# Relaying out the delta rule's diagonal blocks on two DMA queues

## The chip, the cores and the metric

The kernel runs on one core of a Trainium2 chip. The core has five engines with a queue each: TensorE (PE in the profile; its weight loads are PEld), VectorE (DVE), ScalarE (ACT), GpSimd (POOL) and SyncE (SP), and DMA transfers that an engine's queue issues. An engine runs its own queue in order. The metric is the time of one execution in microseconds on the device; the median of repeated runs counts.

## The reference

Two transformer blocks, one after the other, on 512 tokens of width 1024, all in float32. The first block mixes by a gated delta rule (four heads) and a spatial gate, then attends to a memory of 256 rows, then runs an MLP. The second has an mLSTM and window attention, an MLP and a gated embedding. The change lies in the delta rule of the first block. Per head, the reference solves a unit lower triangular system in each chunk of 64 positions:

```python
m = jnp.where(strict, jnp.einsum('bhnid,bhnjd->bhnij', k_beta, k) * lmask, 0.0)
a = m + jnp.eye(c, dtype=f32)
rhs = jnp.concatenate([v_beta, k_beta * jnp.exp(decay)[..., None]], axis=-1)
sol = lax.linalg.triangular_solve(a, rhs, left_side=True, lower=True, unit_diagonal=True)
...
_, o = lax.scan(step, s0, xs)
```

## The kernel before

Every large product of float32 matrices is made of three matmuls on split operands (lines 284, 285 and 286, in the helper `mm3`): a high half rounded to a shorter float type (`wh`, made by a ScalarE cast, line 265) and the rest (`wl`, made by a VectorE subtraction, line 266). `wload` does this for each weight: a DMA on SyncE's queue into `wr` (line 261), the cast, the subtraction. The weights of one projection are two such loads, so TensorE cannot go on with a product before VectorE has made the second `wl`.

The kernel uses chunks of 128 positions for the delta rule, four of them (`NB`), and inverts the unit triangular matrix of each chunk explicitly. `dn_head` does one head in two steps, separated by a `yield`. The first normalises q and k (squares at lines 618 and 621, an inverse root by Newton steps on VectorE at lines 187 to 192), makes the decay factors (636 to 641) and the products `dM` and `QKT` (648, 651). The second inverts: it starts from the 16x16 blocks on the diagonal, 8 in each of 4 chunks, 32 in all.

The diagonal blocks are first gathered by a product with a mask (line 666 with a 16-wide result) and copied by ScalarE to `Lp` (line 676, tile `dVb`), in which the rows of the blocks lie along the 128 partitions. Four DMAs (line 683, one for each chunk) relay them out into `Lb` (in tile `dV`): 32 partitions, one block of 16x16 in each. There VectorE inverts all 32 blocks at once by 15 steps of two small instructions (lines 686 and 688) in `Tb`, and four more DMAs (line 690) bring the result back to the layout along the partitions, `Rp` (tile `dY`). Line 692 reads that into `dTb`. Two rounds of block merging follow (lines 666 four more times a head, 699, 700, 703, 706, 709), then the last merge to 128 (716 to 726), the products with the right sides (612), and a scan over the four chunks (740 to 759).

The four heads run beside the projections of the mixer and, from head 2 on, beside the projections of the memory (`xa_wk`, `xa_wv`), whose keys are made by 256-wide matmuls. The memory's rows come in by DMAs of line 818 on SyncE's queue. After a head, `L778` transposes its output for the projection that follows.

What stands where on each engine is not written out in the kernel. A scheduler sets it when the program is built, from the dependences and its own estimate of what takes how long. So a change of a queue in two lines may move instructions of all engines. At run time the order on an engine is fixed, and an instruction that waits holds what stands behind it.

Of the kernel before, what the change touches and what calls it, by code (L numbers as in the profile page):

```python
# [66 lines left out]
class Kern:  # L67
# [523 lines left out]
    def dn_head(self, h, q, k, v, pr, gate, yb_h, yb_l):  # L591

        nc, mp = self.nc, self.mp
# [81 lines left out]
        Lp, Rp = b32("dVb")[:, :, :16], b32("dY")[:, :, :16]  # L675
# [3 lines left out]
        Lb, Tb, Ob = bl(Vt, 0), bl(Vt, 256), bl(Mo, 0)  # L679
        V.memset(Tb, 0.0)  # L680
        V.memset(flat(Tb)[:, 0::17], 1.0)
        for b in range(NB):
            nc.sync.dma_start(Lb[8 * b:8 * b + 8], Lp[:, b])
        for j in range(15):
            n, m = 15 - j, j + 1
            nc.vector.tensor_tensor(out=Ob[:, :n, :m], in0=Lb[:, m:, j:m].broadcast_to([32, n, m]),
               in1=Tb[:, j:m, :m].broadcast_to([32, n, m]), op=ALU.mult)
            nc.vector.tensor_tensor(out=Tb[:, m:, :m], in0=Tb[:, m:, :m], in1=Ob[:, :n, :m], op=ALU.subtract)
        for b in range(NB):
            nc.sync.dma_start(Rp[:, b], Tb[8 * b:8 * b + 8])  # L690
        T_ = b32("dTb")
        TT(out=split(T_, 16), in0=split(Rp, 16).broadcast_to([P, NB, 2, 16]),
           in1=split(self.bmask("half"), 16).broadcast_to([P, NB, 2, 16]), op=ALU.mult)
# [940 lines left out]
```

## Time and profile before

| | us |
|---|---|
| median of three timed runs | 1692.23 (1691.33 to 1692.98) |
| profiled execution, whole | 1697.81 |
| its span | 1695.9 |
| DMAs of line 683, first and last start | 115.9, 225.5 |
| DMAs of line 690, first and last start | 135.2, 257.2 |
| key projections of the memory begin | 211.3 |

In the profile a row of an engine's timeline gives the start in us, the time taken, engine and line, the operation with the tile it writes and those it reads, shapes, and how many equal ones are merged; what stands in brackets is how long the engine was idle before it and what ended that. A matmul is pipelined, so its time overlaps with the next one's; a float32 matmul that is not split shows as two records. A row of waits gives the total in us, the times and the longest. A row of windows gives the stretch, its length, the busy time of TensorE, its weight loads, VectorE, ScalarE and GpSimd with counts, the granted clock of TensorE, the DMA engines' share and GB/s. "SPq" and "ACTq" are the issues on SyncE's and ScalarE's queues.

### The profile page before, as it was taken

To read this page: it belongs to the slowest core of one execution; us is meant where nothing else is said; L and a number is where in the kernel's file an instruction comes from. 1 tells how busy PE (TensorE), PEld (TensorE's weight loads), DVE (VectorE), ACT (ScalarE), POOL (GpSimd) and SP (SyncE) were. 2 spreads that over 40 slices of the span, in tenths; PEclk is the share of its full clock that TensorE was granted. 3 is DMA by queue.
4 is the path that set the end of the run, shared out by engine and by line. 5 is a ranking of instruction groups with operands and counts; after the bars stand their busy time and mean duration, and the time that the engine had idled before them with its cause. 6 is when DMAs were issued, how large, how long until landed. Compare 5 with 4: busy or idle time off the path is not lost.

```text
span 1695.9 us, 25881 instructions
## 1 busy us (share of the span) xinstructions
PE 1680.3 (99%) x9916; PEld 1462.6 (86%) x9916; DVE 1210.9 (71%) x2521; ACT 823.3 (49%) x1462; POOL 71.9 (4%) x92
## 2 busy tenths in 40 slices
PE   9999999999999999999999999999999999999998
PEld 8988899777898989899999887788888989898987
DVE  6988876756676867688856569865466767676875
ACT  5355745544444444455454457654244444444554
POOL 0200000100000000000000000000000000000000
PEclk9999989999999999999999999999999999999999
DMA  6321347636446464433333332334464464644331
GB/s 204 101 76 52 96 129 179 162 81 171 128 130 169 126 173 120 148 100 98 103 94 106 100 88 69 94 87 112 114 196 121 128 175 124 170 125 141 100 112 50
DMA packets 81947, 205.63 MB, mean 121 GB/s; under 512 B 13088, under 2 KB 14240, under 8 KB 81824
## 3 DMA queue, kind: packets, MB, share of 16 engines
q1 hardware_dynamic: 62672, 169.29, 31.9%
q0 software_dynamic: 9216, 16.78, 7.0%
q10 hardware_dynamic: 9936, 17.91, 3.8%
q8 instruction: 78, 1.28, 0.3%
q14 instruction: 45, 0.37, 0.1%
HBM read 201.59 MB, written 35.65 MB: 140 GB/s over the span
## 4 chain that ended last, share of the span: by engine, by line
PE 90%; DVE 5%; ACT 2%; DMA 1%; issue 1%; SPq 0%; ACTq 0%; DVEq 0%
PE psd L286 21%; PE psd L284 21%; PE psd L285 21%; PE x L284 6%; PE x L285 5%; PE x L286 5%; DVE wl L266 1%; PE c L666 1%; PE c L612 1%; PE lg L1375 1%; PE po L1402 1%; ACT wh L265 1%; DVE S L442 1%; DMA wr<-in_xa_wq_dram 0%; PE c L284 0%
## 5 line engine op out<-in xcount | busy, mean ns | idle before, releaser
L286 PE MATMUL psd<-S,wl 128*128 128x512 f32 (+1 forms) x1256 | 484.1, 386 | 2.7 <-DVE wl L266 2.5
L284 PE MATMUL psd<-S,wh 128*128 128x512 f32 (+1 forms) x1256 | 486.3, 388 | 0.0
L285 PE MATMUL psd<-S,wh 128*128 128x512 f32 (+1 forms) x1192 | 458.5, 385 | 0.5 <-DVE S L330 0.5
L286 PEld LDWEIGHTS psd<-S,wl 128*128 128x128 f32 x1256 | 237.9, 190 | 48.9 <-DVE wl L266 4.3
L284 PEld LDWEIGHTS psd<-S,wh 128*128 128x128 f32 x1256 | 238.5, 190 | 44.5 <-ACT S L326 0.4
L266 DVE TENSOR_TENSOR wl<-wr,wh 128x1024 fp32r<-128x1024 f32 (+2 forms) x160 | 192.1, 1201 | 110.0 <-ACT wh L265 109.2
L285 PEld LDWEIGHTS psd<-S,wh 128*128 128x128 f32 x1192 | 226.1, 190 | 43.3 <-DVE S L330 1.0
L265 ACT CAST wh<-wr 128x1024 fp32r<-128x1024 f32 (+2 forms) x160 | 163.9, 1026 | 149.1 <-PE psd L285 101.2
L284 PE MATMUL psd<-wh,S 128*128 128x256 f32 (+2 forms) x480 | 135.9, 283 | 0.0
L286 PE MATMUL psd<-wh,S 128*128 128x256 f32 (+2 forms) x480 | 135.6, 283 | 0.0
L285 PE MATMUL psd<-wl,S 128*128 128x256 f32 (+2 forms) x480 | 135.5, 282 | 0.0
L284 PE MATMUL x<-S,wh 128*128 128x256 f32 x452 | 129.0, 287 | 0.2
L285 PE MATMUL x<-S,wh 128*128 128x256 f32 x452 | 126.6, 281 | 0.0
L286 PE MATMUL x<-S,wl 128*128 128x256 f32 x452 | 126.0, 280 | 0.0
L284 PE MATMUL psd<-S,whx 128*128 128x512 f32 (+1 forms) x296 | 107.9, 366 | 0.0
L286 PE MATMUL psd<-S,wlx 128*128 128x512 f32 (+1 forms) x296 | 107.5, 364 | 0.0
L285 PE MATMUL psd<-S,whx 128*128 128x512 f32 (+1 forms) x296 | 107.2, 363 | 0.0
L1001 DVE TENSOR_TENSOR x_fm<-x_fm,x 128x256 f32<-128x256 f32 x192 | 79.7, 418 | 24.8 <-PE x L286 23.1
L284 PEld LDWEIGHTS psd<-wh,S 128*128 128x128 f32 x480 | 90.5, 189 | 0.4
L285 PEld LDWEIGHTS psd<-wl,S 128*128 128x128 f32 x480 | 90.4, 188 | 0.3
L284 PE MATMUL x<-S,whx 128*128 128x256 f32 x316 | 90.6, 287 | 0.0
L286 PEld LDWEIGHTS psd<-wh,S 128*128 128x128 f32 x480 | 90.4, 188 | 0.1
(455 smaller groups left out, 3174.7 us busy)
## 6 DMA issues: line engine op xcount, KB each, us to landing
wrx<-in_ffn_w_dram SPq DMA_DIRECT2D x32, 512.0 KB
wrx<-in_w_up_dram SPq DMA_DIRECT2D x20, 512.0 KB
wr<-in_w_in_qk_dram SPq DMA_DIRECT2D x16, 512.0 KB
sums_ffn_w<-in_ffn_w_dram ACTq DMA_DIRECT2D x32, 256.0 KB
wr<-in_ffn_w_dram SPq DMA_DIRECT2D x16, 512.0 KB
sums_w_down<-in_w_down_dram ACTq DMA_DIRECT2D x32, 256.0 KB
wr<-in_w_in_v_dram SPq DMA_DIRECT2D x12, 512.0 KB
wr<-in_w_up_dram SPq DMA_DIRECT2D x12, 512.0 KB
```

The source lines that it names most:

```text
L265: self.last_cast = nc.scalar.copy(hi[:, c], raw[:, c])
L266: nc.vector.tensor_tensor(out=lo[:, c], in0=raw[:, c], in1=hi[:, c].bitcast(F32), op=ALU.subtract)
L284: mm(ps, ah, bh, start=first, stop=False, skip_group_check=more)
L285: mm(ps, ah, bl, start=False, stop=False, skip_group_check=more)
L286: self.last_mm = mm(ps, al, bh, start=False, stop=last, skip_group_check=more)
L442: nc.vector.tensor_scalar(out=d, in0=d, scalar1=ag[:, j, 0:1], scalar2=r[:, j:j + 1], op0=ALU.subtract, op1=ALU.mult)
L612: nc.tensor.matmul(blk(ps, b), lhs(b), rhs(b), start=True, stop=True)
L666: nc.tensor.matmul(ps[:, b * n:(b + 1) * n], lhs[:, b], rhs(b), start=True, stop=True)
L1001: TT(out=x[n][t], in0=x[n][t], in1=ps, op=op)
L1375: nc.tensor.matmul(ps[:, i, K0:], qs[:, 2 * e2 + i, cs], kd[:, w, kc], start=(w == 0), stop=(w == 1))
L1402: nc.tensor.matmul(po, vhl[:, kb, j], pT[:, w], start=(kk == kks[0] and w == 0), stop=(kk == 1 and w == 1))
```

## The change

Of each group of four DMAs, the second and the fourth are issued from ScalarE's queue; the first and the third stay on SyncE's.

```diff
         for b in range(NB):
-            nc.sync.dma_start(Lb[8 * b:8 * b + 8], Lp[:, b])
+            (nc.scalar if b % 2 else nc.sync).dma_start(Lb[8 * b:8 * b + 8], Lp[:, b])
         for j in range(15):
...
         for b in range(NB):
-            nc.sync.dma_start(Rp[:, b], Tb[8 * b:8 * b + 8])
+            (nc.scalar if b % 2 else nc.sync).dma_start(Rp[:, b], Tb[8 * b:8 * b + 8])
```

Nothing is computed otherwise. The scheduler orders TensorE, VectorE, ScalarE and SyncE anew between about 108 and 300 us of the run; GpSimd's order is the same. Two places matter below.

The first is the start of the memory's key projection, beside heads 2 and 3. On SyncE's queue, with `wr` the weights of `xa_wk`, `e` the memory's rows, `dV` and `dY` the relays of head 2 (the last one, `dV_2835`, is head 3's):

```order
 L818 DMA e_491_2705<-in_mem_dram 128x256
 L818 DMA e_493_2712<-in_mem_dram 128x256
-L261 DMA wr_3024<-in_xa_wk_dram 128x1024
+L683 DMA dV_2283<-dVb_399_2280 8x16x16 x2
 L261 DMA wr_3030<-in_xa_wk_dram 128x1024
-L690 DMA dY_400_2281<-dV_2283 128x1x16 x4
 L261 DMA wr_3096<-in_xa_wk_dram 128x1024
-L683 DMA dV_2835<-dVb_518_2832 8x16x16 x4
 L261 DMA wr_3102<-in_xa_wk_dram 128x1024
+L690 DMA dY_400_2281<-dV_2283 128x1x16 x2
+L683 DMA dV_2835<-dVb_518_2832 8x16x16 x2
```

The write-back of head 2 moves from ahead of the weights `wr_3096` and `wr_3102` to behind them; `wr_3024` moves further ahead.

On VectorE at the same place, before; `wl_2756` is the lower half of the second weight of the first key projection, 686 and 688 are the inversion of head 2, whose fifteen steps run from 32x15 over 32x14x2 to 32x15 again:

```order
L686 TENSOR_TENSOR dA_402_2284<-dV_2283 32x3x13
L648 TENSOR_TENSOR dM_2576<-c_462_2571,slg_2546 128x512
L688 TENSOR_TENSOR dV_2283<-dV_2283,dA_402_2284 32x3x13
L651 TENSOR_TENSOR QKT_2583<-c_464_2578,slg_2546 128x512
L686 TENSOR_TENSOR dA_402_2284<-dV_2283 32x2x14
L190 TENSOR_TENSOR rsmt_2726<-rsmy_2725 128x2
L266 TENSOR_TENSOR wl_2756<-wr_2754,wh_2755 128x1024
L688 TENSOR_TENSOR dV_2283<-dV_2283,dA_402_2284 32x2x14
```

and now:

```order
L686 TENSOR_TENSOR dA_402_2284<-dV_2283 32x13x3
L191 SCALAR_TENSOR_TENSOR dot_1873<-dot_1873,dso_1860 128x4
L266 TENSOR_TENSOR wl_2756<-wr_2754,wh_2755 128x1024
L192 SCALAR_TENSOR_TENSOR doy_1872<-dot_1873,doy_1872 128x4
L688 TENSOR_TENSOR dV_2283<-dV_2283,dA_402_2284 32x13x3
L190 TENSOR_TENSOR dot_1873<-doy_1872 128x4
L475 TENSOR_TENSOR x_fm<-psd_2648,x_fm 128x512
```

The weight's lower half moves from the fourteenth step of the inversion to the third, and with it ahead of head 3's factors (641) and products (648, 651). `wl_3026` and `wl_3032`, the two of the second key projection, move from behind the inversion to its tenth and eleventh steps; `wl_3098`, of the third, stands behind the first L700 of head 2 in both orders, but now ahead of the L706 that follows, where the second L700 stood ahead of it.

The second place is head 2's write-back on ScalarE. `wh` are casts of weights, `S_503` the keys' high half, `vt` head 3's scaled values, `S_176` head 1's output, `dVb_518` head 3's diagonal blocks:

```order
 L643 ACTIVATE kdec_2561<-c_450_2515,dkd_2542 128x128 x3
+L265 CAST wh_3097<-wr_3096 128x1024
+L326 CAST S_503_2745<-e_514_2814 128x256
+L690 DMA dY_400_2281<-dV_2283 128x1x16 x2
 L643 ACTIVATE vt_2563<-c_466_2585,dvi_2544 128x128 x4
+L265 CAST wh_3103<-wr_3102 128x1024
 L329 ACTIVATE S_176_1231<-c_515_2818,vec 128x512
 L676 COPY dVb_518_2832<-c_517_2827 128x4x16
```

The two write-backs come in ahead of head 3's `vt`, and the casts of the third key projection's weights move from behind L676 to around them.

On TensorE, the groups of head 2's merging (L666, four products each; tiles `c`) stand among the key projection's matmuls (`psd`). Two of them before:

```order
L286 MATMUL psd_3065<-S_477_2662,wl_3026 128x256
L666 MATMUL c_407_2339<-dY_406_2337,dV_2283 128x32 x4
L284 MATMUL psd_3065<-S_477_2662,wh_3025 128x256
L285 MATMUL psd_3065<-S_478_2663,wh_3025 128x256
L286 MATMUL psd_3065<-S_477_2662,wl_3026 128x256
L284 MATMUL psd_3065<-S_477_2662,wh_3025 128x256
L285 MATMUL psd_3065<-S_478_2663,wh_3025 128x256
L286 MATMUL psd_3065<-S_477_2662,wl_3026 128x256
L284 MATMUL psd_3065<-S_477_2662,wh_3025 128x256
L666 MATMUL c_408_2345<-dTb_403_2325,dA_402_2284 128x32 x4
```

and now:

```order
L285 MATMUL psd_3137<-S_478_2663,wh_3097 128x256
L666 MATMUL c_407_2339<-dY_406_2337,dV_2283 128x32 x4
L286 MATMUL psd_3108<-S_477_2662,wl_3098 128x256
L284 MATMUL psd_3108<-S_477_2662,wh_3097 128x256
L285 MATMUL psd_3108<-S_478_2663,wh_3097 128x256
L666 MATMUL c_408_2345<-dTb_403_2325,dA_402_2284 128x32 x4
L286 MATMUL psd_3108<-S_477_2662,wl_3098 128x256
```

Between the two stand three matmuls where seven stood. In the whole run of head 3's first group (`c_517`, 16 wide) and head 2's four (`c_404`, `c_407`, `c_408`, `c_411`), the matmuls between neighbours are 4, 8, 3 and 10 now, and were 14, 11, 7 and 10; the transposes of L778 stand four matmuls ahead of `c_517` now, and stood next to it.

## The prediction

> **What bounds the kernel now.** I read the page first: busy shares, granted clock, chain.
>
> ```profile
> span 1695.9 us, 25881 instructions
> PE 1680.3 (99%) x9916; PEld 1462.6 (86%) x9916; DVE 1210.9 (71%) x2521; ACT 823.3 (49%) x1462; POOL 71.9 (4%) x92
> ...
> PEclk9999989999999999999999999999999999999999
> ...
> PE 90%; DVE 5%; ACT 2%; DMA 1%; issue 1%; SPq 0%; ACTq 0%; DVEq 0%
> ```
>
> TensorE works 1680.3 of 1695.9 us and carries 90% of the chain. The change removes no TensorE instruction. It can move the time in two ways only: through the 15.6 us in which TensorE stands, and through the one slice in which the clock digit is 8. So I asked for TensorE's own waits, and for the stretch around that digit in order of time.
>
> ```profile
> PE psd L286 <- DVE wl L266: 2.5, 3, 1.2
> ...
> PE c L666 <- DVE dTb L692: 0.2, 1, 0.2
> ```
>
> ```profile
> 214.52 1.15 PE L612 MATMUL c<-dq,dk 128*128 128x128 f32 x8
> 215.43 0.36 PE L284 MATMUL psd<-S,wh 128*128 128x256 f32 x1
> ...
> 217.74 0.39 PE L286 MATMUL psd<-S,wl 128*128 128x256 f32 x1 [1.16 <-DVE wl L266]
> ...
> 219.25 0.28 PE L285 MATMUL psd<-S,wh 128*128 128x256 f32 x1
> 219.37 0.28 PE L286 MATMUL psd<-S,wl 128*128 128x256 f32 x1
> ...
> 220.20 0.60 PE L778 MATMUL c<-masks,do 128*128 128x128 f32 x4
> 220.63 0.96 PE L666 MATMUL c<-masks,dT 128*128 128x16 f32 x8
> 221.44 0.36 PE L286 MATMUL psd<-S,wl 128*128 128x256 f32 x1
> ...
> 224.38 0.38 PE L286 MATMUL psd<-S,wl 128*128 128x256 f32 x1 [0.88 <-DVE wl L266]
> ...
> 224.74 1.08 PE L666 MATMUL c<-dTb,dT 128*128 128x32 f32 x8
> 225.65 0.39 PE L285 MATMUL psd<-S,wh 128*128 128x256 f32 x1
> ...
> 227.97 1.75 PE L666 MATMUL c<-dY,dV 128*128 128x32 f32 x8
> ```
>
> ```profile
> 210.00:220.00 10.00, 8.84 (x74) 8.57 (x74) 9.78 (x57) 4.29 (x13) 0.82 (x1) 1.00 0.30 65
> 222.20:225.60 3.40, 2.52 (x20) 2.10 (x18) 3.33 (x9) 1.38 (x3) 0.00 (x0) 1.00 0.47 157
> 225.60:239.20 13.60, 13.60 (x66) 13.60 (x66) 5.92 (x18) 4.50 (x10) 0.81 (x1) 0.51 0.46 119
> ```
>
> The first number is a start; the difference of two starts is what a row costs in a full stream (219.25 to 219.37: 0.12 us for a 256-wide matmul; 224.74 to 225.65: 0.91 for a group of four L666 products; 220.63 to 221.44: 0.81 for the 16-wide group; 220.20 to 220.63: 0.43 for four transposes; 214.52 to 215.43: 0.91 for four 128-wide products). Two waits of 1.16 and 0.88 us, both for the lower half of a split weight (`wl`, L266), fall into the key projection of the memory, beside head 2's inverse. VectorE, which makes `wl`, is busy 9.78 of 10 us there: it is late because it is full. Right after the second wait the granted clock drops to 0.51 for 13.6 us: (1 - 0.51) x 13.6 = 6.7 us lost. So this stretch holds 2.04 us of waits and 6.7 us of clock; that is what the change can win.
>
> **The change part by part.** Its direct effect is on 32 small transfers.
>
> ```profile
> L690 SPq DMA_DIRECT2D dY<-dV x16: 604/648/1817, 135.2 to 257.2; - x16
> ```
>
> ```profile
> 218.97 3.90 SPq L690 DMA_DIRECT2D dY<-dV  x4
> 223.04 0.34 SPq L261 DMA_DIRECT2D wr<-in_xa_wk_dram  x1
> ```
>
> ```profile
> 206.30 0.50 ACTq L226 DMA_DIRECT2D sums_ffn_w<-in_ffn_w_dram  x1
> 206.47 0.26 ACT L621 ACTIVATE c<-c 128x128 f32<-128x128 f32 x1
> ```
>
> One issue takes 0.648 us of SyncE. Two of four moved make each of the eight relays 2 x 0.648 = 1.3 us shorter. That is 10.4 us over all eight, none of it on TensorE's path: heads 0 to 3 run beside projections, and a reader of a relay (L692 to L666) kept TensorE waiting once, for 0.2 us. I cost it at zero; if the cover were gone it would be at most the 1.3 us of one relay at a time.
>
> ScalarE takes 16 issues in return. No row shows such a transfer on its queue; the nearest are 0.50 us for L226 there and 0.648 on SyncE, 8 to 10.4 us in all. An activation starts at 206.47 while L226's issue runs to 206.80, so an issue need not stop the engine; ScalarE is busy 49%. I take zero, bounds 0 and 1.3 us for the one place where ScalarE's work is next on TensorE's path (the slower rival).
>
> [...]
>
> What counts is the order that the shorter relays give to the engines.
>
> ```profile
> 213.47 0.33 DVE L641 SCALAR_TENSOR_TENSOR slg<-slg,ds,masks 128x128 f32<-128x128 f32 x1
> 213.73 0.20 DVE L688 TENSOR_TENSOR dV<-dV,dA 32x55 f32<-32x55 f32 x1
> ...
> 214.99 0.69 DVE L648 TENSOR_TENSOR dM<-c,slg 128x512 f32<-128x512 f32 x1
> 215.59 0.18 DVE L688 TENSOR_TENSOR dV<-dV,dA 32x39 f32<-32x39 f32 x1
> 215.71 0.69 DVE L651 TENSOR_TENSOR QKT<-c,slg 128x512 f32<-128x512 f32 x1
> ...
> 216.41 0.14 DVE L190 TENSOR_TENSOR rsmt<-rsmy 128x2 f32<-128x2 f32 x1
> 216.48 1.21 DVE L266 TENSOR_TENSOR wl<-wr,wh 128x1024 fp32r<-128x1024 f32 x1
> ...
> 218.81 0.10 DVE L688 TENSOR_TENSOR dV<-dV,dA 32x15 f32<-32x15 f32 x1
> ...
> 224.39 0.29 DVE L692 TENSOR_TENSOR dTb<-dY,masks 128x128 f32<-128x128 f32 x1
> ```
>
> By starts, an L641 costs 0.26 us, an L648, L651 or L475 0.6, an L686 or L688 about 0.13, one of the tiny ones (L187 to L192 and the like) 0.07. In the new order 60 VectorE instructions that stood ahead of `wl_2756` (the wait at 217.74) stand behind it: 22 of L686 and L688 (2.9 us), four L641 (1.0), L648, L651 and L475 (1.8), and 31 tiny ones (2.2). That is 7.9 us; two memsets (0.3) come ahead. On TensorE, what stood ahead of its first use shrinks by 16 matmuls of 0.12, three groups of 0.91 and the transposes of L606 (0.4): 5.1 us. Its margin grows by 7.6 - 5.1 = 2.5 us, more than the 1.16 it was late. For `wl_3032` (the wait at 224.38) VectorE sheds 5.8 us net and TensorE 2.6: 3.2 us of margin against 0.88. SyncE's issue at 223.04, a weight held up behind head 2's write-back, now stands ahead of it too. **Both waits go: -2.04 us.**
>
> What is late next is `wl_3098`. VectorE now makes it two places behind L700 (one L828 of 0.35, then 1.14), and TensorE wants it directly behind the group that itself needs L700 (0.91). If that group starts just as L700 ends, TensorE waits 0.35 + 1.14 - 0.91 = 0.6 us; if VectorE is ahead, nothing. I take **+0.5 us** (bounds 0, and 2.0 if as much is lost as now).
>
> Whether the clock falls again is the large question. Head 2's small groups stand closer: from the four transposes of L778 to the end of the last of five L666 groups there are 29 matmuls, 29 x 0.12 + 0.43 + 0.81 + 4 x 0.91 = 8.4 us, and 4.9 of these, 58%, are groups that stream little. Before the fall, of 222.2 to 225.6, wait, group and the two transposes of L360 took 0.88 + 0.91 + 0.2 of 3.4 us: also 58%. Head 1, where the clock held:
>
> ```profile
> 178.17 1.08 PE L666 MATMUL c<-dTb,dT 128*128 128x32 f32 x8
> ...
> 185.34 0.97 PE L666 MATMUL c<-dY,dV 128*128 128x32 f32 x8
> ```
>
> four groups and one of transposes in 8.1 us, (4 x 0.91 + 0.43) / 8.1 = 50%. The limit lies between; the new place is on the falling side. I let the fall **stay: 0** (bounds -6.7 and +6.7, gone or twice as long).
>
> Sum against the profiled execution's 1697.81 us (span and 1.9 around it): 1697.81 - 2.04 + 0.5 = 1696.3. The median of the timed runs is 5.6 us lower, at 1692.23; carried over, **1690.7 us**. Two runs are told from no change at about 0.2%, 3.4 us: this forecast is "same".
>
> **Rivals.** *A, the clock holds.* With the waits gone, no single place of the run has idle time and groups together; both earlier heads kept their clock. Against it: the 58%. It gives 1692.23 - 2.04 - 6.7 = 1683.5. [...]
>
> *B, slower: ScalarE waits.* At head 2 its two write-backs wait for VectorE's last L688; behind them on ScalarE stand `vt` (four scalings), the cast `wh_3103`, L329, L676 and L703, whose result the second L666 group reads:
>
> ```profile
> 216.50 1.14 ACT L643 ACTIVATE vt<-c,dvi 128x128 f32<-128x128 f32 x4 [2.04 <-PE c L606]
> 220.83 0.69 ACT L329 ACTIVATE S<-c,vec 128x512 fp32r<-128x512 f32 x1 [3.19 <-PE c L778]
> ...
> 221.74 1.05 ACT L265 CAST wh<-wr 128x1024 fp32r<-128x1024 f32 x1
> ```
>
> From the last L688 this path is about 1.3 (two issues) + 1.1 + 1.1 + 0.7 us, and some 0.4 for the two small copies: 4.6 us. Now that L688 ends at 218.9 and the group starts at 227.97; at full clock and without the wait that would be 226.8 - 0.9, 7.0 us later. The order adds 3.0 us of TensorE's work and 1.6 of VectorE's: 8.4 us against 4.6. It decides once the recursion ends nearly 4 us later than that; then TensorE idles amid the groups and the low clock lasts about twice as long: 1690.7 + 6.7 = 1697.4.
>
> *C, the relays get no shorter*, since their landing, not their issue, holds them. The order is fixed when the program is built, so the first two waits still go, and one relay 1.3 us late may show: 1692.23 - 2.04 + 1.3 = 1691.5.
>
> **How the numbers follow.** Forecast 0.45, A 0.30, B 0.13, C 0.12. Forecast and C are "same": 0.57; A is faster, 0.30; B slower, 0.13. The range runs from A's 1683.5, rounded down to 1683, to 1696, which takes the waits at their upper bound and a fall half as long again; B is left out. The likeliest case alone reaches from 1689 to 1694.
>
> **What would show it.** Right: no wait of L286 for `wl` over 0.5 us in the key projection, the chain of waits still 90% TensorE, one digit below 9 in the clock row, some 3 us later than now, with matmuls of 0.21 us between starts. Wrong: a clock row of nines (A); idle of TensorE at L666 for L703 or L692, and ScalarE idle before `vt` (B); issues of L683 and L690 that still take over 2 us from first to first reader with TensorE waiting at L666 (C). A fall beside head 0 or 1 would refute the 50 to 58%.

## The result, and the profile after

| | before | after |
|---|---|---|
| median of the runs, us | 1692.38 (1691.33 to 1692.98, 4 runs) | 1703.62 (1703.09 to 1704.51, 4 runs) |
| ratio of after to before | | 1.0069 (95% interval 1.0058 to 1.0081) |
| profiled execution, us | 1697.81 | 1704.51 |

The change makes the kernel slower by 0.7%, 11 us. I had forecast 1690.7 and a range of 1683 to 1696. First the page of the kernel after: span, busy time, granted clock in 40 slices, chain.

```profile
span 1702.7 us, 25884 instructions
...
PE 1682.9 (99%) x9916; PEld 1463.5 (86%) x9916; DVE 1210.6 (71%) x2521; ACT 823.7 (48%) x1462; POOL 71.9 (4%) x92
...
PEclk9999989999999999999999999999999999999999
...
PE 87%; DVE 7%; ACT 2%; DMA 2%; issue 1%; ACTq 0%; DVEq 0%; SPq 0%
```

It looks like the page before: TensorE carries the chain, one clock digit is below 9. Idle time of TensorE rose from 15.6 to 19.8 us. Its waits (total, times, longest) and three stretches of windows (the figure behind the five busy times is the granted clock):

```profile
PE c L666 <- DVE dTb L692: 2.3, 2, 2.0
PE c L666 <- ACT vt L643: 1.2, 1, 1.2
...
PE c L753 <- ACT do L755: 0.9, 1, 0.9
...
PE c L666 <- DVE doy L192: 0.8, 1, 0.8
...
PE psd L286 <- DVE wl L266: 0.7, 2, 0.5
```

```profile
180.00:190.00 10.00, 7.99 (x38) 6.50 (x38) 5.60 (x14) 5.14 (x19) 1.02 (x1) 0.83 0.53 123
230.00:240.00 10.00, 9.53 (x51) 9.33 (x52) 7.15 (x16) 3.04 (x8) 0.40 (x1) 0.63 0.40 97
240.00:250.00 10.00, 10.00 (x66) 9.21 (x65) 3.92 (x15) 4.11 (x8) 0.41 (x1) 0.69 0.36 81
```

The waits for `wl` went from 2.5 to 0.7 us, as forecast. New are a wait of 2.0 us for head 1's relay (L692), one of 1.2 us for `vt` at head 2, and two of 0.9 and 0.8 behind 240 us. And the clock is low at two places: beside head 1 (0.83 in 180 to 190) and beside head 2.

Head 1 in the timeline of after, queues, VectorE and TensorE together:

```profile
176.25 0.33 SPq L261 DMA_DIRECT2D wr<-in_xa_wk_dram  x1
...
176.54 1.36 ACTq L690 DMA_DIRECT2D dY<-dV  x2
...
176.68 1.44 SPq L690 DMA_DIRECT2D dY<-dV  x2
...
183.24 0.29 DVE L692 TENSOR_TENSOR dTb<-dY,masks 128x128 f32<-128x128 f32 x1 [2.29 <-DMA dY<-dV]
...
183.59 1.08 PE L666 MATMUL c<-dTb,dT 128*128 128x32 f32 x8 [2.01 <-DVE dTb L692]
```

All four write-backs were issued by 178.1, and the last of them landed only at 183.1. Ahead of SyncE's two stands a 512 KB weight, which the scheduler had put behind them before:

```profile
173.44 2.67 SPq L690 DMA_DIRECT2D dY<-dV  x4
...
176.71 1.56 SPq L261 DMA_DIRECT2D wr<-in_xa_wk_dram  x2
```

Head 2, first ScalarE, then TensorE:

```profile
227.43 1.05 ACT L265 CAST wh<-wr 128x1024 fp32r<-128x1024 f32 x1 [2.42 <-PE c L606]
227.53 1.45 ACTq L690 DMA_DIRECT2D dY<-dV  x2
228.38 0.40 ACT L326 CAST S<-e 128x256 fp32r<-128x256 f32 x1
229.03 1.14 ACT L643 ACTIVATE vt<-c,dvi 128x128 f32<-128x128 f32 x4 [0.24 <-issue]
```

```profile
230.22 1.06 PE L666 MATMUL c<-masks,dT 128*128 128x16 f32 x8 [1.22 <-ACT vt L643]
...
232.09 1.46 PE L666 MATMUL c<-dTb,dT 128*128 128x32 f32 x8 [0.25 <-DVE dTb L692]
```

ScalarE is idle until 227.43, and from there runs a cast, a second cast and `vt`, for which TensorE waits.

### The profile page after: what moved, and what is told of

The parts are those of the page before. It is cut to its first block, busy times and chain, and to the rows that moved or that the text cites. A ratio compares the mean times of both kernels' runs of the same rounds, so it can differ in the third digit from the quotient of the medians.

```text
span 1702.7 us, 25884 instructions
## 1 busy us (share of the span) xinstructions
PE 1682.9 (99%) x9916; PEld 1463.5 (86%) x9916; DVE 1210.6 (71%) x2521; ACT 823.7 (48%) x1462; POOL 71.9 (4%) x92
## 4 chain that ended last, share of the span: by engine, by line
PE 87%; DVE 7%; ACT 2%; DMA 2%; issue 1%; ACTq 0%; DVEq 0%; SPq 0%
PE psd L286 20%; PE psd L285 20%; PE psd L284 20%; PE x L284 6%; PE x L285 5%; PE x L286 5%; DVE wl L266 2%; PE c L666 1%; ACT wh L265 1%; PE c L612 1%; DMA wr<-in_xa_wv_dram 1%; PE lg L1375 1%; PE po L1402 1%; DVE S L442 1%; DMA dY<-dV 1%
```

## The experiments

Four theories stood against each other. **1**: ScalarE is held at head 2 by its two write-backs; TensorE waits for `vt`, and the clock falls. **2**: head 1's write-backs land late because a weight load stands ahead of them on SyncE's queue. **3**: the fall comes from the small groups of head 2 standing closer. **4**: a relay on two queues lands later in itself. Apart from these stood the question how often the kernel before has the fall that its first profile shows. Each ratio is to runs of before of the same round, whose medians are 1691.06 to 1691.68 us.

| kernel | median, us | range (runs) | ratio to before, 95% interval |
|---|---|---|---|
| before_again | 1691.44 | 1689.52 to 1694.08 (10) | 1.0000, 0.9991 to 1.0009 |
| gather2 | 1693.99 | 1692.59 to 1700.51 (10) | 1.0021, 1.0011 to 1.0031 |
| back2 | 1695.92 | 1692.60 to 1698.83 (10) | 1.0028, 1.0019 to 1.0038 |
| back2_not2 | 1702.68 | 1696.57 to 1704.72 (4) | 1.0063, 1.0041 to 1.0084 |
| fixA | 1702.17 | 1701.27 to 1704.68 (4) | 1.0063, 1.0048 to 1.0079 |
| fixB | 1699.87 | 1696.16 to 1706.89 (6) | 1.0058, 1.0038 to 1.0078 |
| fixAB | 1695.87 | 1693.82 to 1699.71 (10) | 1.0026, 1.0016 to 1.0035 |
| after_x | 1704.21 | 1701.96 to 1705.65 (4) | 1.0071, 1.0049 to 1.0092 |
| pool2 | 1704.95 | 1704.29 to 1705.42 (4) | 1.0074, 1.0059 to 1.0089 |
| g_pool | 1693.31 | 1690.88 to 1699.44 (10) | 1.0013, 0.9999 to 1.0027 |

### The kernel before, once more

No edit.

> The kernel before, once more, to see in how many of its runs the granted clock falls at head 2. Theory 'fall is the difference': the fall of 13.6 us (6.7 us of time) that the first profiled execution of before shows (1697.81 us) is absent in its ordinary runs; most runs then give 1691 to 1693 us with spans near 1690 and a listed clock above 0.995, and a profile taken in such a run has 0.9 or more in every window of 220:240. Theory 'offset': every run of before has the fall and profiled executions are longer by a constant 5.6 us; then a profiled run gives 1697 to 1698 again, the timed ones 1692, and the listed clock is 0.995 for all.

Its page:

```profile
span 1687.7 us, 25881 instructions
...
PE 1673.0 (99%) x9916; PEld 1456.2 (86%) x9916; DVE 1210.4 (72%) x2521; ACT 823.1 (49%) x1462; POOL 71.9 (4%) x92
...
PEclk9999999999999999999999999999999999999999
```

Nines throughout, and an execution of 1689.52 us: the fall is absent here. The ten runs stay below 1694.1; the first profiled execution, with the fall, took 1697.81, which is 6.8 us above the 1691.0 that it would have taken without. Each run also lists its mean granted clock, which the fall of the first profile brings down to 0.995. Of 63 runs of before (these ten, and 53 beside the other kernels) one looks like it, with 0.996 and 1696.77 us; the others list 0.998 to 1.000. So the ordinary run of before has no fall, and the offset that I had taken for constant was the fall.

From here the sum can be made on profiles: 1702.7 - 1687.7 = 15.0 us. The trace lists the granted clock with exact bounds (times from the span's start):

```
kernel         clock 0.5 from   for (us)
before         225.87           13.653
before_again   none
after          184.84            3.413
after          232.63           13.653
```

After's 17.07 us at half clock cost 8.5; TensorE's idle time grew from 14.7 to 19.8, 5.1; 1.4 us remain, and by the rows that TensorE had streamed by then the two executions are 1.5 us apart at 100 us, ahead of the first relay. Beside the medians of their own runs, before_again's profile is 1.9 us short and after's 0.9 long, which takes the 15.0 to the 11 or 12 us between medians.

### One half of the change at a time

```diff
 gather2: only line 683 split over both queues
 back2:   only line 690 split over both queues
 back2_not2: the change, but
-            (nc.scalar if b % 2 else nc.sync).dma_start(Rp[:, b], ...)
+            (nc.scalar if b % 2 and h != 2 else nc.sync).dma_start(Rp[:, b], ...)
```

> Only the gathers (L683) split over both queues, the write-backs (L690) all on SyncE, head 1's ahead of the weight load wr_2748 and head 2's ahead of wr_3096. Theory 1 (ScalarE is held at head 2 by its two write-backs, TensorE then waits for vt and the clock falls): nothing is left of the loss, 1688 to 1693 us, no wait of L666 for vt over 0.3 us. Theory 2 (head 1's write-backs stand behind a weight load and land 5 us late): also no loss, since they stand ahead of it here; no wait of L666 for dTb over 0.5 us at head 1. Theory 4 (a relay on two queues lands later by itself): part of the loss stays, 1695 or more, with L688 waiting for the gather.

> Only the write-backs (L690) split, the gathers all on SyncE; on ScalarE head 2's two write-backs stand behind vt here, not ahead of it, and on SyncE head 1's stand ahead of wr_2748. Theory 1: vt isn't held, no wait for it, no fall: 1688 to 1693 us. Theory 2: no wait for dTb at head 1, the 2.3 us there are gone. Theory 4 (write-backs on two queues land late in themselves): L692 waits for its DMA over 2 us at heads 1 and 2, TensorE with it, 1697 to 1704 us.

> The change, but head 2's four write-backs all on SyncE; up to head 2 every queue has the order of the change, head 1's write-backs behind wr_2748. Theory 1: TensorE's wait for vt at head 2 (1.2 us) goes, and with it the fall (6.7): 1694 to 1697 us, while the 2 us at head 1 stay. Theory 2 alone (head 1's late landing is what costs, through idle there or a clock that is low from there): 1702 to 1704 as the change. Theory 3 (the fall comes from the small groups standing closer, whatever ScalarE does): the fall stays, 1701 to 1703.

Waits of TensorE from 160 to 300 us, of gather2, of back2 and of back2_not2, and a window at each head of the last:

```profile
PE c L666 <- DVE dTb L692: 1.5, 2, 0.9
```

```profile
PE c L666 <- DVE dTb L692: 0.6, 1, 0.6
```

```profile
PE c L666 <- DVE dTb L692: 2.3, 1, 2.3
...
PE c L666 <- DVE dT L670: 0.9, 1, 0.9
```

```profile
181.00:184.50 3.50, 1.24 (x10) 0.80 (x7) 0.95 (x4) 0.77 (x4) 0.91 (x1) 1.00 0.60 213
226.00:234.00 8.00, 6.78 (x56) 6.31 (x54) 6.21 (x14) 5.11 (x12) 0.27 (x1) 1.00 0.34 60
```

Either half alone costs 3 to 5 us by the medians, with no wait for the relay at head 1, where the write-backs stand ahead of the weight. By theories 1 and 2 nothing of the loss would be left here, so something else of the new orders costs too, and what it is stays open. By theory 4 TensorE would wait over 2 us at heads 1 and 2 of back2, and the time would be 1697 us or more: its wait for the relay is 0.6 us, at head 2 alone, and the median 1695.92, though two of ten runs are over 1697. The third kernel has the wait of head 1 in full and none for `vt` (0.9 us for `dT` stands at that group), and yet three of its four runs take 1701.83 to 1704.72; only the profiled one, at 1696.57, kept its clock. The three left no trace, but list a mean clock of 0.994 and 0.995, as the change does. So a loss of clock of that size does not need ScalarE's write-backs at head 2: theory 1 was not enough.

### Holding one instruction in its place

The scheduler takes an order between two instructions of one engine that is not a wait. With it each suspect could be put back, and the rest left to the change.

```diff
 fixA (line 261): on SyncE, wr_2748 is issued behind head 1's write-backs
-            nc.sync.dma_start(raw[:, c], src[:, c])
+            with self.tc.issue_after(after.ins) if after else nullcontext():
+                nc.sync.dma_start(raw[:, c], src[:, c])
 fixB (line 643): on ScalarE, head 2's write-backs are issued behind head 3's vt
+        if h == 3:
+            for b in (1, 3):
+                self.tc.add_manual_dep(self.relay[2, b].ins, last.ins.name, ...)
 fixAB: both
```

> The change, with one thing held: the memory's first key weight (wr_2748) is issued on SyncE behind head 1's write-backs instead of ahead of them. Head 2 keeps its hold (ScalarE's two write-backs ahead of vt). Theory 2 (the weight load ahead on the same queue makes head 1's write-backs land 5 us late): L692 at head 1 reads within 4.5 us of the first write-back's issue instead of 6.6, TensorE's wait of 2.0 us there goes, and with it the one low window at 185 (1.7 us): 3 to 4 us less than the change, 1699 to 1701 us. Rival (landing is slow on two queues by itself): L692 still 6 us after, 1702 to 1704. Theory 1 says the wait for vt and the long fall at head 2 stay.

> The change, with one thing held: ScalarE issues head 2's two write-backs behind vt (L643 of head 3) instead of ahead of it. Everything up to head 2 is as in the change. Theory 1 (ScalarE held at head 2 makes TensorE wait for vt, and the poor window there makes the clock fall for 13.6 us): the wait for vt goes; the long fall goes or gets rarer: 1695 to 1698 us. The 2.0 us at head 1 and the low window there stay. Theory 3 (the fall at head 2 comes from the order of the small groups, not from ScalarE): the fall stays, 1702 to 1704.

> Both holds together. If theories 1 and 2 account for the whole loss, this gives the time of the kernel before or a little less, 1688 to 1693 us, with no wait of L666 over 0.5 us at heads 1 and 2 and no low window. If something else of the new order costs (as 3 to 5 us did in the kernels with one half of the change), 1694 to 1697 us. If the relays on two queues are themselves late, 1699 or more.

**fixA.** Head 1 in its timeline (lines are shifted by 1 to 3; L695 is the L692 of the change, L668 its L666):

```profile
176.93 1.37 SPq L692 DMA_DIRECT2D dY<-dV  x2
176.93 1.35 ACTq L692 DMA_DIRECT2D dY<-dV  x2
...
178.98 0.85 SPq L262 DMA_DIRECT2D wr<-in_xa_wk_dram  x2
...
180.60 0.28 DVE L695 TENSOR_TENSOR dTb<-dY,masks 128x128 f32<-128x128 f32 x1
...
181.01 1.00 PE L668 MATMUL c<-dTb,dT 128*128 128x32 f32 x8
```

3.7 us from the first issue to the reader instead of 6.7, and no wait. The packets of the transfers say why (64-byte packets are the relay's, 256 on each queue):

```
kernel  queue    first start   last end (us)
after   ScalarE  179.04        179.98
after   SyncE    179.16        182.65     (behind wr_2748, whose packets start at 177.21)
fixA    ScalarE  178.25        179.28
fixA    SyncE    178.44        179.40
```

The two kernels differ in more than the queue: the DMA engines were 76 to 94% busy from 179 to 183 us in the change, and 28% in fixA while the relay's packets ran. But within the change both halves met the same busy engines, and the half on ScalarE's queue landed by 180.0; only the half behind the weight on SyncE's queue was 2.7 us later. Theory 2 holds, and theory 4 falls: from its first packet to its last the relay on two queues took 1.15 us in fixA, and in the change 0.93 on ScalarE's queue against 3.49 behind the 512 KB load on SyncE's. The gain in time was missed, though (1699 to 1701 us expected), and the wait for `vt`, which I had expected to stay, is gone: TensorE waits for `kdec` at head 2 instead, in a changed order (its longest wait: total, times, longest),

```profile
PE c L614 <- ACT kdec L645: 2.5, 1, 2.5
```

and the clock falls there for 3.4 and 10.2 us: 1702.17 us. A hold moves the other instructions too.

**fixB.** Its ScalarE at head 2, and two windows:

```profile
227.73 1.05 ACT L265 CAST wh<-wr 128x1024 fp32r<-128x1024 f32 x1 [2.24 <-DMA wr<-in_xa_wk_dram]
...
228.99 1.13 ACT L643 ACTIVATE vt<-c,dvi 128x128 f32<-128x128 f32 x4
```

```profile
181.50:190.00 8.50, 7.33 (x27) 6.47 (x28) 4.17 (x9) 4.77 (x17) 1.02 (x1) 0.60 0.34 71
228.00:235.00 7.00, 5.78 (x48) 5.40 (x48) 5.30 (x13) 4.27 (x10) 0.00 (x0) 1.00 0.48 70
```

`vt` starts at 228.99, behind a cast that waited for its weight; in the change it starts at 229.03. So the write-backs had held ScalarE by next to nothing (0.24 us in its row), and what holds `vt` is the cast ahead of it. In the change, too, that cast waited for its weight, whose last part landed at 227.35; its row names the L606 that ended at the same time. Theory 1's mechanism falls, though the clock did hold at head 2 in this execution: in the new order the L666 groups of head 2 that need the relay stand several projection matmuls further back, and no window there is that poor. That speaks for theory 3, but does not show it: the median, 1699.87, lies between the ranges of theory 1 (1695 to 1698) and theory 3 (1702 to 1704), and four of the six runs list a mean clock of 0.992 to 0.996, with no trace of where it fell. At head 1, where the order is that of the change, TensorE waited 2.5 us for the relay, and the clock fell for 6.8 us.

**fixAB.** No wait at head 1, one at head 2 (the row below, of TensorE's waits), no low window in the profile ahead of the run's last microseconds, and the slowest of ten runs is below all the runs of the change:

```profile
PE c L614 <- ACT kdec L645: 1.2, 1, 1.2
```

It takes back 8 of 12 us. 4 us over before remain, as the case expected in which something else of the new order costs. In its profile they are 2.8 us past the first 100 us, in small pieces, and which rows they come from I have not settled. In four of the ten runs the clock has a part in it: they list 0.997 or 0.998, and three of them are the slowest, 1697.91 to 1699.71.

### Where the clock falls

The low stretches that end within the run measure 3.413 us and 13.653 (4.00 times as long) in before and after, 17.0 in after_x (5 times); in after the two start 47.79 us apart, 14.00 times 3.413. So I cut each profile into windows of 3.413 us, a grid through the start of its low stretch; the grid lies 0.6 us from a multiple of 3.413 in before, 0.5 in after, 2.9 in after_x. For each window I counted the rows that TensorE streams in it (the columns of its matmuls, spread evenly over the time of each record). A probe without the model:

```python
def run(k, w=P):                 # k matmuls of 512 columns, then a copy that the next unit waits for
    for _ in range(k):
        nc.tensor.matmul(pa, X, R, start=True, stop=True)
    nc.vector.tensor_copy(out=X[:, :w], in_=pa[:, :w])
for k in (6, 4, 3, 2, 1): ...    # units of run(k) for some 17 us, then run(88)
for n in (256, 128, 64, 32, 16): # float32 matmuls of n columns without a wait, then run(88)
    small(KS[n], n); run(88)
```

> A probe that leaves the whole model out and writes a tile of copies: stretches of some 17 us on TensorE between full stretches of 34 us. First five rungs in which TensorE waits for a copy of VectorE after every 6, 4, 3, 2 and 1 matmuls of 512 columns (idle of about half a us each time, never 3.4 us long), then five without waits, of matmuls of 256, 128, 64, 32 and 16 columns one behind another. Theory 'columns per window' (the clock falls after a window of 3.413 us in which fewer than about 2500 columns are streamed, the full stretch streams some 4500): it falls on rungs of both kinds where the windows hold fewer than that, whatever the idle time is. Theory 'idle window' (it falls only after a whole idle window): no fall on any rung. Theory 'idle share': it falls on rungs with waits only, never on those without.

Windows of the probe (no ScalarE column): a full one; units of two matmuls; the first window of units of one; what follows it; 64 columns; the first window with 32 columns; what follows it.

```profile
81.22:84.63 3.41, 3.41 (x16) 2.83 (x16) 0.00 (x0) 0.00 (x0) 1.00 0.00 0
132.42:135.83 3.41, 2.26 (x8) 0.89 (x6) 0.88 (x3) 0.00 (x0) 1.00 0.00 0
163.14:166.55 3.41, 1.87 (x5) 0.74 (x4) 1.17 (x4) 0.00 (x0) 1.00 0.00 0
166.55:187.03 20.48, 14.34 (x21) 6.14 (x21) 4.67 (x16) 0.00 (x0) 0.50 0.00 1
268.95:272.37 3.42, 3.42 (x33) 3.42 (x32) 0.00 (x0) 0.00 (x0) 1.00 0.02 5
299.67:303.09 3.42, 2.96 (x23) 2.50 (x22) 0.36 (x2) 0.00 (x0) 1.00 0.00 0
303.09:326.98 23.89, 23.89 (x114) 23.89 (x114) 0.00 (x0) 0.00 (x0) 0.50 0.00 1
```

The clock falls on the rung whose single waits are 0.4 us long, and on the two of 32 and 16 columns, which have no wait but the one ahead of their first matmul: the window before the fall is 87% busy, and with TensorE 100% busy the clock then stays low to the end of the rung. It holds at 66% busy (units of two). So neither a whole idle window nor the idle share sorts these rungs. A full window streams 7,700 rows here, not the 4,500 that I had expected (those were records of the kernel's projections, f32 records counted once). A record of an unsplit float32 matmul takes about as long as a split one of twice the columns: between starts at full clock, medians in before, 258 unsplit columns take 0.217 us and 512 split ones 0.232, 128 unsplit 0.111 and 256 split 0.118; 32 and 16 unsplit take 0.112. With its columns counted twice, the probe and twelve profiles of the kernel, some 1,200 windows (the kernel's in the first 320 us, the probe's up to its last matmul), give:

```
full clock, and the next window falls        full clock, and it holds
after       181.43   1090                    gather2      223.92  3074
fixA        234.24   1505                    back2_not2   182.82  3076
after       229.21   1526                    back2_not2   230.60  3128
fixA        224.00   1664                    probe        135.83  3154
probe       163.14   1907                    probe        132.42  3192
after_x     228.17   2201
probe       350.87   2222                    half clock: the highest that stays low   3118
fixB        178.96   2573                                the lowest that rises        3149
probe       299.67   2860
before      222.45   2950
pool2       220.42   3096
```

All eleven falls come after windows of at most 3,096 rows, and no window at full clock with more was followed by one; below that only two held, at 3,074 and 3,076. At half clock the highest count with which it stayed low and the lowest with which it rose lie at the same place, 3,118 and 3,149. Busy time does not sort the falls, as a pair of windows shows, the first of gather2 and the second of after:

```profile
223.92:227.33 3.41, 1.67 (x12) 1.47 (x12) 1.79 (x6) 0.37 (x1) 0.00 (x0) 1.00 0.27 36
```

```profile
229.21:232.63 3.42, 2.16 (x17) 1.96 (x17) 1.92 (x7) 2.58 (x7) 0.00 (x0) 1.00 0.48 74
```

TensorE is busy 49% of the first, with 256-wide matmuls, and the clock holds; it is busy 63% of the second, two thirds of it in groups of 16 and 32 columns, and the clock falls. The weight of two was chosen because the falls and the rises then part near one count. For the falls alone every weight from 1.4 to 1.9 parts them from all windows that held as well. So the 3,100 is my estimate from these profiles, good to a tenth or so, and what the hardware itself counts is not shown. The windows before a fall were busy 55 to 87% in the probe (1.87 and 2.96 of 3.41 us), none of them idle.

An estimate of how other executions may go can be made from the profiles by these counts: slide the grid over one and see at how many of the offsets some window has under 3,072 rows (10 to 320 us). before_again: 5%; fixAB and g_pool: none; gather2 and back2: none, but just 3,072 at about 15 and 11% of the offsets; back2_not2: 99%. In the change, head 1 alone gives 88%, and with head 2 up to its fall it is 98%. This takes the waits of one execution for all, and that is too little: the poorest window of fixAB's profile holds some 3,900 rows, yet its two runs near 1699.5 list a mean clock of 0.997 and 0.998, and the four slowest of g_pool 0.995 to 0.998, where the profiles without a fall have 0.999 or 1.000. So the waits of other executions differ from the profiled one's.

> The change once more, for a second profile in which the 3.413-us grid of the clock lies elsewhere. If a window falls whenever TensorE streams less than some 3070 rows in it (f32 matmuls counted twice; from the falls so far between 2950 and 3074), the first profile's starts of poor windows (180.1 to 183.2 and 227.6 on, 3.0 us and over 3.4 us wide, of a grid of 3.4) give a fall at head 2 in every run and one at head 1 in nine of ten: both again here, 1702 to 1705 us. If the falls are chance, this profile lacks one, and the times spread over 8 us as those of the versions with a hold did.

```profile
231.58:248.60 17.02, 17.02 (x81) 16.41 (x79) 8.87 (x26) 3.94 (x12) 0.81 (x1) 0.50 0.38 95
180.00:190.00 10.00, 7.78 (x47) 6.43 (x46) 6.33 (x13) 4.95 (x20) 1.02 (x1) 1.00 0.68 143
```

The change again, with the waits of 2.2 and 1.3 us. This time the grid lies 2.4 us further along: head 2 falls for five windows, and head 1's poor stretch (807 rows in its worst 3.4 us) lies across two windows, neither of which has under 3,072 rows. Eight of eight runs of the change take 1701.96 to 1705.65 us. My nine in ten for head 1 missed this one; the offset of this profile says why.

### Relays on GpSimd

```diff
 pool2:  (nc.gpsimd if b % 2 else nc.sync) in lines 683 and 690
 g_pool: nc.gpsimd in line 683, nc.sync in line 690
```

> The relays split between SyncE and GpSimd instead of SyncE and ScalarE. ScalarE has its order of before, head 1's write-backs stand ahead of wr_2748 on SyncE. If ScalarE's issues and the weight load are what cost, this gives 1689 to 1693 us, no fall at head 1 or 2 but by chance, perhaps a little under the kernel before. If a relay on two queues, or GpSimd's own issue (some 0.8 to 1.0 us each in its rows so far), makes the write-backs late: L666 waits for dTb by 1 to 2 us at heads 1 or 2, 1694 to 1700.

> All gathers (L683) on GpSimd, all write-backs on SyncE ahead of the weight loads, nothing on ScalarE. If only the write-backs' landing and ScalarE's order matter, 1689 to 1693 us; if the gather on GpSimd starts the recursion later than SyncE did (four issues of 0.8 to 1.0 us against 0.65), VectorE's recursion at head 2 ends 1 to 2 us later and L666 waits for dTb there, as in the kernel with the gathers on both queues: 1693 to 1695.

pool2 missed its main case (up to 1693 us) by 12 us and the rival named beside it (up to 1700) by 5. Its write-backs at head 2 and their reader:

```profile
220.79 1.37 SPq L690 DMA_DIRECT2D dY<-dV  x2
221.33 1.23 POOL L690 DMA_DIRECT2D dY<-dV  x2 [10.77 <-PE c L606]
...
225.40 0.29 DVE L692 TENSOR_TENSOR dTb<-dY,masks 128x128 f32<-128x128 f32 x1 [1.07 <-DMA dY<-dV]
```

The window from 220.42, with a wait of 0.7 us and a 16-wide group, streams 3,096 rows, and the clock falls for five windows, 17.1 us; 2.1 us of waiting for this reader lie in the first of them. ScalarE issues none of it. g_pool, with the write-backs all on SyncE and ahead of the weights, cannot be told from before by its interval; its poorest window holds 3,170 rows, 2% over the highest that fell, and five of ten runs are over 1694 us. None of the versions beats the kernel before.

## Why the prediction was wrong

**TensorE as the bound**, and the waits and the clock as the only places to win or lose: right.

**The two waits for `wl` go, -2.04**: right, 2.5 us before and 0.7 after. **A new wait of +0.5 for `wl_3098`**: right in size, the longest left is 0.5.

**"I let the fall stay: 0"**, and with it **"carried over, 1690.7"**: this is the step that failed. That the clock would fall again at head 2 was right; that the small groups alone bring it about is not shown, since a wait of 1.2 us stood in the same window. But the fall of the profile was no part of the median: 1697.81 - 6.7 is 1691.1, within 1.1 us of the median, and before_again, without a fall, shows it. The sum started from a profile with the fall and ended at a median without it, so that a new fall cost nothing. With the fall charged at the 6.8 us that it costs, the same steps give 1692.23 - 2.04 + 0.5 + 6.8 = 1697.5. For the same reason the rival in which the clock holds could not reach 1683.5: 1690.7 was its time.

**"None of it on TensorE's path: I cost it at zero"** (the relays): wrong at head 1. I had looked at what SyncE's queue holds behind head 2's write-backs, not at what the new order put ahead of head 1's. It cost 2.0 us of waiting, and in the first profile a window at half clock, 1.7: 1701.2. I had named a fall beside head 0 or 1 as what would refute the 50 and 58%; it came, after a window of 1,090 rows, and in these profiles the rows in a window sort the falls, as the share of small groups does not.

**ScalarE's 16 issues at zero**: close, 0.24 us where it was to matter. **The slower rival** had the wait (for `vt`, 1.2 us) and the sign, with 1697.4 us and 0.13. Its mechanism was not what ran: the cast ahead of `vt` waited for its weight until 227.4, and the L688 that the write-backs need had ended at 225.9. With 1.2 the sum is 1702.4, and with the new 0.9 for `do` and 0.8 for `doy` 1704.1, against 1703.6 measured; that it comes so near is in part luck, since the small pieces that fixAB left open are not in it.

**The third rival**, relays no shorter, had the right event (a late landing) with the wrong place and price: 1.3 us at one wait, none for the clock.

## What to carry to other kernels

Where a profiled execution lies outside the range of the timed runs, find the event that makes it so before any sum is made, and ask in what share of the runs it occurs. Where a chain of small matmuls runs beside a projection, count the rows that TensorE streams in the poorest 3.4 us, not its busy time: here waits of 0.7 to 2 us stood in windows of 1,090 to 3,096 rows, and brought 1.7 to 8.5 us of clock on top. The mean clock that each run lists tells in how many runs it fell. And read what a new order puts ahead of a small transfer on its queue, at each place and not at the one with the largest wait.

## What the hardware showed unasked

The granted clock went to 0.5 for stretches of 3.413 us or multiples of it. All eleven falls of the thirteen profiles came after windows of 1,090 to 3,096 rows by the count above, at most 40% of the 7,700 of a full one in the probe; two windows of 3,074 and 3,076 held. By its profiles the kernel before lost 0 or 6.8 us to such stretches, the change 8.5 in both, as one and four windows or as five. A write-back of 16 KB behind a 512 KB load on SyncE's queue ended 2.7 us later than its other half on ScalarE's. And in after ScalarE's queue issued two DMAs while an earlier activation still ran (the write-backs at 227.53 beside the cast of 227.43 and 1.05 us), and a later one waited 0.24 us for an issue.
